# An encoder layer on one core: the attention's output product as seven block products in place of eight, with the sums in DRAM replanned

## The chip, the cores and the metric

The kernel runs on one core of one Trainium2 chip. The metric is device time in microseconds (us), the median of several runs of the same program. The program's text runs once and is scheduled ahead of time into one instruction stream per engine: PE (matmuls), DVE and ACT (elementwise work), POOL and SP (here mostly issuing transfers). Streams run in order and wait for each other by semaphores.

## The reference

A bidirectional encoder layer on 512 tokens of width 1024, all in float32: a state-space branch and a gated branch are merged, then comes cross-attention to 256 memory tokens, then a SwiGLU feed-forward part (FFN) of width 2816 and a last norm. What the change touches is the end of the attention:

```python
def memory_cross_attention(hn, memn, w_q, w_k, w_v, w_o):
    q = (hn @ w_q).reshape(bsz, seq, XATTN_HEADS, XATTN_HEAD_DIM)      # 4 heads of 256
    ...
    p = jax.nn.softmax(s, axis=-1)
    o = jnp.einsum('bhlm,bmhd->blhd', p, v).reshape(bsz, seq, D_MODEL)
    return o @ w_o                                                     # w_xo, 1024 x 1024

h = h + memory_cross_attention(rms_norm(h, xattn_norm_g[i]), memn, w_q[i], w_k[i], w_v[i], w_xo[i])
h = h + swiglu(rms_norm(h, ffn_norm_g[i]), w_gate[i], w_up[i], w_down[i])
```

## The kernel before

**Products.** PE multiplies a reduced float32 type. Every operand is therefore split into a high part (a cast, on ACT) and a low part (the rest, by a subtraction on DVE); `split` does both, at lines 85 and 86. `mm3` (line 358) then issues three matmuls: high by high, high by low, low by high. Weights are split on the chip as they come: a load of 512 KB by SP into `wraw` (three buffers), then `whi` on ACT and `wlo` on DVE (three buffers each).

**The plan.** All weight pieces stand in one list, `plan`, in the order of their use. `next_w` hands out the next piece, starts the load of the piece three places ahead (`LOADS`) and splits up to two places ahead (`SPLITS`). Program order comes from this; a scheduler then orders each engine's stream by its own estimate of when things are ready.

**Strassen's products before the change.** `w_proj_b`, `w_q`, most of `w_gate` and `w_up` (in units of 512 columns) and `w_down` are already computed as block products of seven for eight: tokens, rows and columns of the weight are halved, seven products of sums of blocks are formed instead of eight of blocks, and their results are added up. Four of the seven need a sum of weight blocks. For `w_proj_b`, `w_q` and `w_down` these sums (`bsum`, `qsum`, `dsum`) are made in DRAM, long before they are used: `plan_sums` hangs each job on two places of the plan, at the first a copy of one block by SP (line 274), some places later a second transfer, issued by POOL, that adds the other block onto it (line 275). The numbers in `plan_sums([...])` are these places and distances.

**`w_xo` before.** It is an ordinary product. `values` makes one head's attention output (two tiles `po`) and splits it into `ot_hi` and `ot_lo`. `tokm(w_xo, 0, ...)` computes the first 512 columns for all four token tiles, with the values of heads 1 to 3 hooked in between its weights. The loops over `t0` behind it compute the other 512 columns, two token tiles at a time. `add_evac` adds each result onto `h`, sums its squares on ACT, and for the second half starts the FFN's norm of that token tile (`feat_norm`, `norm_feat`): two scalings `xs` (line 512), transposes on PE (`ptr`, line 520), and the split into `fn`.

**The FFN's start** takes tokens 0 and 1 first (`gate_part(0, T0)`, a unit's first product, `gate_part(1, T0)`, a unit's second), then tokens 2 and 3. T0 and T1 are the halves of the tokens, K0 and K1 those of the rows.

Of the kernel before, what the change touches and what calls it, by code (L numbers as in the profile page):

```python
# [9 lines left out]
F32 = mybir.dt.float32  # L10
# [42 lines left out]
def hybrid_layer_kernel(  # L53
# [173 lines left out]

    def plan_units(units, down):
# [28 lines left out]
    def plan_sums(places):  # L257
# [1141 lines left out]
    def values(hd, p_hi, p_lo):  # L1399
        for dt_ in range(2):  # L1400
# [4 lines left out]
            split(ot_hi[:, 2 * hd + dt_, :], ot_lo[:, 2 * hd + dt_, :], ps)  # L1405
# [49 lines left out]
    ot_lo = slot("E", (P, KD, T), F32R, "ot_lo")  # L1455
    values(0, *pts.pop(0))
    probs2 = scores(2)
    probs3 = scores(3)
    turn(1, probs1)

    def second():
        values(1, *pts.pop(1))
        turn(2, probs2)
        turn(3, probs3)

    def last_two():
        for i in (2, 3):
            values(i, *pts.pop(i))

    g_f = gain(ffn_norm_g[0], "g_f")  # L1470
    ot = (ot_hi, ot_lo)
    fn_hi, fn_lo = token_slot("fn", AWAY)
    fn = (fn_hi, fn_lo)

    tokm(w_xo, 0, ot, KD, add_evac(0, 1, None), hooks={1: second, 2: last_two})
# [6 lines left out]
    full = fp.tile([P, KD, T], F32, tag="full", name="full", bufs=1)  # L1482


    fin = add_evac(1, 1, feat_norm(g_f, fn_hi, fn_lo, full))
    held = []
    for t0 in (0, 2):
        ps = {t: bank(f"pt{t - t0}") for t in (t0, t0 + 1)}
        for wi in range(2):
            if t0 == 0:  # L1490
                held.append((wi,) + next_w(w_xo, 2 * wi, 2, 512, 512))
            for t in ps:
                tok_block(ps[t], t, held[wi:wi + 1], ot, 2, slice(0, 512), wi == 0, False)
            tick(2.7)
        if t0 == 0:
            held += [(wi,) + next_w(w_xo, 2 * wi, 2, 512, 512) for wi in (2, 3)]
        for t in ps:
            tok_block(ps[t], t, held[2:4], ot, 2, slice(0, 512), False, True)
            fin(t, ps[t])
            tick(2.7)  # L1500
# [308 lines left out]
```

## Time and profile before

| | |
|---|---|
| median of 3 runs | 892.44 us (892.33 to 893.95) |
| the profiled execution | 893.12 us, of which its span is 891.3 us |
| PE, busy share of the span | 99% |
| DVE, ACT, POOL | 72%, 55%, 12% |
| granted TensorE clock, mean | 0.997 |
| DMA | 165.36 MB, 186 GB/s on average |

A row of the chain of waits has start, length and what the chain was in. A row of the timeline has engine, line, operation, output and inputs, shape and count, and in brackets the idle time ahead of it with what ended it. A group row ends in busy us, mean ns of one, and idle time ahead of the group with what ended it. PEld is the loading of a matmul's stationary side, beside PE.

### The profile page before, as it was taken

How to read it: one execution, taken by the hardware profiler on the slowest of the kernel's cores; microseconds unless marked ns; L12 is line 12 of the kernel's file. 1: busy time of each engine (PE TensorE's matmuls, PEld its weight loads, DVE VectorE, ACT ScalarE, POOL GpSimd, SP SyncE). 2: the span in 40 equal slices, each digit the busy share in tenths (PEclk: the TensorE clock that was granted, in tenths of full speed). 3: DMA queues.
4: the chain of work that ended last, by engine and by line, in shares of the span. 5: the costliest groups of instructions: out<-in, count | busy, mean ns of one | idle time of the engine just before them, and what ended most of it. 6: DMA issues, size and time to landing. Idle time of an engine off the chain costs nothing.

```text
span 891.3 us, 14796 instructions
## 1 busy us (share of the span) xinstructions
PE 881.1 (99%) x5744; PEld 788.0 (88%) x5744; DVE 642.5 (72%) x1048; ACT 487.4 (55%) x714; POOL 106.9 (12%) x165
## 2 busy tenths in 40 slices
PE   9999999999999999999999999999999999999996
PEld 6788888888889998889899978999999999988875
DVE  5697653889847368658856836676878777899875
ACT  5743994244396254347656534645555455655664
POOL 1005301111032111001001001101121111000010
PEclk9999999999999999999999999999999999999998
DMA  8667456978533789834579747627899999356672
GB/s 255 196 189 182 114 155 177 189 191 190 159 87 84 212 285 268 288 117 140 168 221 256 194 103 197 166 81 181 213 237 233 216 225 249 95 167 207 204 230 102
DMA packets 118408, 165.36 MB, mean 186 GB/s; under 512 B 11825, under 2 KB 84161, under 8 KB 118210
## 3 DMA queue, kind: packets, MB, share of 16 engines
q1 hardware_dynamic: 97474, 135.74, 47.9%
q0 software_dynamic: 20576, 28.15, 19.9%
q8 instruction: 45, 0.74, 0.3%
q10 hardware_dynamic: 288, 0.52, 0.2%
q14 instruction: 25, 0.20, 0.1%
HBM read 157.61 MB, written 46.63 MB: 229 GB/s over the span
## 4 chain that ended last, share of the span: by engine, by line
PE 97%; DMA 1%; SPq 1%; ACT 0%; DVE 0%; issue 0%; POOLq 0%; ACTq 0%
PE pf L358 26%; PE pt L358 17%; PE px L1110 12%; PE dx L358 6%; PE pq L1110 6%; PE dq L358 3%; PE pv L1110 3%; PE bx L1110 3%; PE qx L1110 2%; PE dv L358 2%; PE pz L871 2%; PE pk L814 2%; PE bq L1110 1%; PE qv L1110 1%; PE psc L358 1%; PE qq L1110 1%
## 5 line engine op out<-in xcount | busy, mean ns | idle before, releaser
L86 DVE TENSOR_TENSOR wlo<-wraw,whi 128x1024 fp32r<-128x1024 f32 (+1 forms) x145 | 172.2, 1189 | 101.2 <-ACT whi L85 101.0
L85 ACT CAST whi<-wraw 128x1024 fp32r<-128x1024 f32 (+1 forms) x145 | 148.6, 1026 | 152.2 <-PE pf L358 44.0
L358 PE MATMUL pf<-xn,whi 128*128 128x512 f32 x448 | 139.6, 391 | 0.0
L358 PEld LDWEIGHTS pf<-xn,whi 128*128 128x128 f32 x448 | 83.7, 188 | 17.0
L358 PE MATMUL pf<-xn,wlo 128*128 128x512 f32 x224 | 87.3, 390 | 0.0
L1110 PE MATMUL px<-fn,whi 128*128 128x256 f32 x480 | 83.4, 277 | 0.0
L1110 PEld LDWEIGHTS px<-fn,whi 128*128 128x128 f32 x480 | 72.7, 188 | 0.2
L85 ACT CAST whi<-b 128x1024 fp32r<-128x1024 f32 x40 | 42.2, 1055 | 50.4 <-PE px L1110 27.4
L86 DVE TENSOR_TENSOR wlo<-b,whi 128x1024 fp32r<-128x1024 f32 x40 | 48.9, 1223 | 27.0 <-ACT whi L85 27.0
L1110 PE MATMUL px<-fn,wlo 128*128 128x256 f32 x240 | 66.4, 277 | 0.0
L1110 PE MATMUL pq<-s,whi 128*128 128x256 f32 x320 | 55.0, 276 | 0.0
L358 PE MATMUL dx<-whi,s 128*128 128x512 f32 x170 | 53.4, 390 | 0.4 <-DVE h L1734 0.4
L85 ACT CAST whi<-t 128x1024 fp32r<-128x1024 f32 x30 | 31.6, 1054 | 35.6 <-PE pv L1110 12.4
L86 DVE TENSOR_TENSOR wlo<-t,whi 128x1024 fp32r<-128x1024 f32 x30 | 36.7, 1225 | 19.7 <-ACT whi L85 19.7
L358 PEld LDWEIGHTS pf<-xn,wlo 128*128 128x128 f32 x224 | 42.1, 188 | 8.7
L1110 PEld LDWEIGHTS pq<-s,whi 128*128 128x128 f32 x320 | 48.3, 188 | 0.0
L1110 PEld LDWEIGHTS px<-fn,wlo 128*128 128x128 f32 x240 | 45.1, 188 | 0.0
L358 PE MATMUL pt<-whi,xn 128*128 128x512 f32 x128 | 43.7, 412 | 0.7 <-ACT xn L85 0.7
L1110 PE MATMUL pq<-s,wlo 128*128 128x256 f32 x160 | 44.2, 276 | 0.0
L358 PEld LDWEIGHTS dx<-whi,s 128*128 128x128 f32 x170 | 31.8, 188 | 7.5 <-issue 0.8
L358 PE MATMUL dx<-wlo,s 128*128 128x512 f32 x85 | 33.0, 390 | 0.0
L275 POOL DMA_DIRECT2D dsum<-in_w_down_dram x12 | 13.3, 1105 | 162.4 <-DMA dsum<-in_w_down_dram 162.4
(453 smaller groups left out, 2296.8 us busy)
## 6 DMA issues: line engine op xcount, KB each, us to landing
wraw<-in_w_in_dram SPq DMA_DIRECT2D x36, 512.0 KB, 4.7
dsum<-in_w_down_dram SPq DMA_DIRECT2D x20, 512.0 KB, 5.4
wraw<-dsum SPq DMA_DIRECT2D x20, 512.0 KB, 4.1
b<-in_w_gate_dram SPq DMA_DIRECT2D x15, 512.0 KB, 5.4
b<-in_w_up_dram SPq DMA_DIRECT2D x15, 512.0 KB, 5.3
wraw<-in_w_down_dram SPq DMA_DIRECT2D x15, 512.0 KB, 4.4
dsum<-in_w_down_dram POOLq DMA_DIRECT2D x10, 512.0 KB, 8.1
dsum<-dsum POOLq DMA_DIRECT2D x10, 512.0 KB, 8.5
```

Of the source, the lines that this page charges most:

```text
L85: hi = nc.scalar.copy(dst_hi, src)
L86: lo = nc.vector.tensor_tensor(dst_lo, src, dst_hi.bitcast(F32), ALU.subtract)
L275: plan[j + step][1].append((0, lambda d=dst, x=more: nc.gpsimd.dma_start(d, x, accum_op=ALU.add)))
L358: m = nc.tensor.matmul(ps, a[x], b[y], start=start and i == 0, stop=stop and i == 2, skip_group_check=free)
L814: nc.tensor.matmul(ps[32 * j:32 * j + 32, q, :], bd[i][:, g].rearrange("p d c -> p (d c)"), lc(es[i], g), start=(i == 0), stop=False, tile ...
L871: nc.tensor.matmul(ps[:, g, :], wt[:, g, :], u[:, o * GO + g, :], start=True, stop=True)
L1110: nc.tensor.matmul(ps[:, j, :], a[x], b[y], start=start and j == k == i == 0, stop=k == 3 and i == 2, skip_group_check=True)
```

## The change

`w_xo` becomes a block product of seven for eight over all 1024 columns. `plan_xo` puts 14 pieces of 512 KB into the plan in place of 8: for each of the products 1 to 7 two pieces (`c` = 0, 1) of 256 rows by 512 columns. Products 1, 2 and 3 read blocks of `w_xo`; 4 to 7 read sums `xsum`, made in DRAM by eight new jobs of `plan_sums`. The places of all sums are written anew: the last two of `w_q`'s come earlier, `w_xo`'s take the places that held `w_q`'s last and `w_down`'s first, three of `w_down`'s are beside `w_xo`, 15 in the FFN's units and six (those of product 4) at the places of `w_down` itself. The order of `w_down`'s sums of products 6 and 7 is exchanged.

On the side of the tokens, `values` now copies `po` to a float32 tile `of` on ACT, and `attention_part` makes the operands of the products from it: after heads 0 and 1 those of products 1 and 7, after heads 2 and 3 those of 6, 5, 4, 2 and, later, 3, with four sums or differences per pair of heads on DVE. `xo_product` multiplies one piece with two token tiles; products 1 and 7 stand between the heads' values. `onto` adds a finished product onto two token tiles of one half of `h`. The FFN's norm of tokens 0 and 1 is started after product 4, that of tokens 2 and 3 after product 3, the last. The memory of the keys (`kt_hi`, `kt_lo`) takes the operands of products 5 and 6.

```diff
+    XSRC = {1: (0, 0), 2: (1, 0), 3: (1, 1)}
+    xsum = {q: dp.tile([P, KD // 2, 512], F32, name=f"xsum{q}") for q in (4, 5, 6, 7)}
+    XO = ((1, 0), (7, 0), (1, 1), (7, 1), (6, 0), (5, 0), (6, 1), (5, 1), (4, 0), (4, 1), (2, 0), (2, 1), (3, 0), (3, 1))
+    def xo_block(i, j, c):
+        return block(w_xo, 4 * i + 2 * c, 2, 512 * j, 512)
+    def plan_xo():
+        for q, c in XO:
+            ...
+                got["raw"] = wp.tile([P, 2, 512], F32, tag="raw", name="wraw", bufs=3)
+                nc.sync.dma_start(got["raw"], xo_block(*XSRC[q], c) if q in XSRC else xo_sum(q, c))
...
-        for q, i, jc, more in ((5, 0, 0, lambda c: down_block(0, 1, c)), (7, 0, 1, lambda c: down_block(1, 1, c)),
-                               (6, 1, 1, lambda c: down_sum(5, c)), (4, 1, 0, lambda c: down_sum(6, c))):
+        for q, first, more in ((5, (0, 0), lambda c: xo_block(0, 1, c)), (7, (0, 1), lambda c: xo_block(1, 1, c)),
+                               (6, (1, 1), lambda c: xo_sum(5, c)), (4, (1, 0), lambda c: xo_sum(6, c))):
+            for c in range(2):
+                jobs.append((xo_sum(q, c), xo_block(*first, c), more(c)))
+        for q, i, jc, more in ((5, 0, 0, lambda c: down_block(0, 1, c)), (6, 1, 1, lambda c: down_sum(5, c)),
+                               (7, 0, 1, lambda c: down_block(1, 1, c)), (4, 1, 0, lambda c: down_sum(6, c))):
...
-    plan_tok(w_xo, 0, KD)
-    for i in range(4):
-        plan_block(w_xo, 2 * i, 2, 512, 512, place=(None, None, 2, 4)[i])
+    plan_xo()
...
-    plan_sums([(5, 3), (7, 3), (9, 2), (13, 5), (14, 5), (16, 4)] + [(18 + 2 * i, 3) for i in range(8)] +
-              [(51 + 2 * i, 2) for i in range(4)] + [(85 + 3 * i, 3) for i in range(3)] +
-              [(95 + 2 * i, 2) for i in range(3)] + [(122 + 4 * i, 4) for i in range(16)])
+    plan_sums([(5, 3), (7, 3), (9, 2), (13, 5), (14, 5), (16, 4)] + [(18 + 2 * i, 3) for i in range(5)] +
+              [(i, 3) for i in (28, 29, 31, 32, 34)] + [(51 + 2 * i, 2) for i in range(4)] +
+              [(i, 3) for i in (67, 74, 82, 87, 91, 95, 99)] + [(124 + 4 * i, 4) for i in range(15)] +
+              [(184 + 5 * i, 4) for i in range(6)])
...
-            split(ot_hi[:, 2 * hd + dt_, :], ot_lo[:, 2 * hd + dt_, :], ps)
+            nc.scalar.copy(of[:, 2 * hd + dt_, :], ps)
+        attention_part(hd)
...
+    xops = {1: ot_q(K0, T1), 2: ot_q(K1, T1), 4: ot_q(K1, T0), 7: ot_q(K0, T0), 3: ot_q(K0, T1)}
+    def attention_part(hd):
+        ...
+        if hd < 2:
+            operand(1, a11)
+            s3_ = np_.tile([P, 2, 256], F32, tag="ev", name="s3", bufs=2)
+            nc.vector.tensor_tensor(s3_, a11, a21, ALU.subtract)
+            operand(7, s3_)
+            return
+        nc.vector.tensor_tensor(a21, a21, a22, ALU.subtract)
+        nc.vector.tensor_tensor(a11, a21, a11, ALU.subtract)
+        operand(6, a11)
+        operand(5, a21)
+        operand(4, a22)
+        operand(2, a12)
+        nc.vector.tensor_tensor(a12, a12, a11, ALU.add)
+        later(2, lambda: operand(3, a12))
...
-    tokm(w_xo, 0, ot, KD, add_evac(0, 1, None), hooks={1: second, 2: last_two})
+    ox = [bank("ox0"), bank("ox1")]
+    xo_product(ox, 1, 0, True, False)
+    values(1, *pts.pop(1))
+    turn(2, probs2)
+    oy = [bank("oy0"), aux("oy1")]
+    xo_product(oy, 7, 0, True, False)
+    values(2, *pts.pop(2))
+    turn(3, probs3)
+    xo_product(ox, 1, 1, False, True)
+    onto(ox, 2, 0, ALU.add)
+    values(3, *pts.pop(3))
+    xo_product(oy, 7, 1, False, True)
+    onto(oy, 0, 1, ALU.subtract)
+    oq = [bank("oq0"), bank("oq1")]
+    xo_product(ox, 6, 0, False, False)
+    xo_product(oq, 5, 0, True, False)
+    xo_product(ox, 6, 1, False, True)
+    onto(ox, 0, 1, ALU.subtract)
+    xo_product(oq, 5, 1, False, True)
...
+    onto(oq, 0, 1, ALU.add)
+    onto(ox, 0, 0, ALU.add)
+    ...
+    onto(ox, 2, 1, ALU.subtract)
+    xo_product(oy, 4, 0, False, False)
+    xo_product(oy, 4, 1, False, True)
+    ...
+    for t in range(2):
+        hs = h[:, t, HALF[0]]
+        nc.vector.tensor_tensor(hs, hs, oy[t], ALU.add)
+        half_done(t, 0)
+        to_fn(t, hss[:, 1, t, :])
+    ov = [bank("ov0"), bank("ov1")]
+    xo_product(ov, 2, 0, True, False)
+    xo_product(ov, 2, 1, False, True)
+    onto(ov, 2, 0, ALU.add)
+    ...
+    for t in range(2):
+        for c in range(2):
+            xo_product(oq, 3, c, False, c == 1, ws[c], (t,))
+        hs = h[:, 2 + t, HALF[1]]
+        nc.vector.tensor_tensor(hs, hs, oq[t], ALU.add)
+        half_done(2 + t, 1)
+        to_fn(2 + t, hss[:, 1, 2 + t, :])
```

More of the change, by code (lines that the diff above doesn't have):

```diff
@@ L1455, in hybrid_layer_kernel, with operand, xo_product, onto @@
     ot_lo = slot("E", (P, KD, T), F32R, "ot_lo")
+    of = slot("B", (P, KD, T), F32, "of")
+    ot_q = lambda ks, ts: (ot_hi[:, ks, ts], ot_lo[:, ks, ts])
+    xops = {1: ot_q(K0, T1), 2: ot_q(K1, T1), 4: ot_q(K1, T0), 7: ot_q(K0, T0), 3: ot_q(K0, T1)}
+    def attention_part(hd):
+        u = slice(2 * (hd % 2), 2 * (hd % 2) + 2)
+        lw = slice(u.start + 4, u.stop + 4)
+        a11, a12, a21, a22 = (of[:, k, t] for t in (T1, T0) for k in (u, lw))
+        def operand(q, src):
+            split(xops[q][0][:, u], xops[q][1][:, u], src)
+        if hd < 2:
[12 more added lines that the diff above has]
+        later(2, lambda: operand(3, a12))
+    g_f = gain(ffn_norm_g[0], "g_f")
+    def xo_product(ps, q, c, start, stop, w=None, ts=(0, 1)):
+        hi, lo = w or next_w(w_xo, q, c)
+        a = xops[q]
+        for t in ts:
+            tsl = slice(t * P, (t + 1) * P)
+            for k in range(2):
+                mm3(ps[t], (a[0][:, 2 * c + k, tsl], a[1][:, 2 * c + k, tsl]), (hi[:, k, :], lo[:, k, :]),
+                    start and k == 0, stop and k == 1, True)
+        tick(1.35 * len(ts))
+    def onto(ps, t0, half, op):
+        for t in range(2):
+            hs = h[:, t0 + t, HALF[half]]
+            nc.vector.tensor_tensor(hs, hs, ps[t], op)
+    def half_done(t, half):
+        sum_sq(hss[:, 1, t, half:half + 1], h[:, t, HALF[half]])
     values(0, *pts.pop(0))
@@ L1458, in hybrid_layer_kernel @@
     probs3 = scores(3)
+    for q, nm in ((5, "kt_hi"), (6, "kt_lo")):
+        s_ = ap_.tile([P, KD, M], F32R, name=nm).rearrange("p (i k) t -> p i k t", i=2)
+        xops[q] = s_[:, 0], s_[:, 1]
     turn(1, probs1)
[L1461 to L1473, printed above, removed]
-    tokm(w_xo, 0, ot, KD, add_evac(0, 1, None), hooks={1: second, 2: last_two})
+    ox = [bank("ox0"), bank("ox1")]
[17 more added lines that the diff above has]
+    xo_product(oq, 5, 1, False, True)
     at.close()
@@ L1482, in hybrid_layer_kernel @@
     full = fp.tile([P, KD, T], F32, tag="full", name="full", bufs=1)
[L1485 to L1500, printed above, removed]
+    onto(oq, 0, 1, ALU.add)
+    onto(ox, 0, 0, ALU.add)
+    for t in range(2):
+        half_done(t, 1)
+    onto(ox, 2, 1, ALU.subtract)
+    xo_product(oy, 4, 0, False, False)
+    xo_product(oy, 4, 1, False, True)
+    fn_hi, fn_lo = token_slot("fn", AWAY)
+    fn = (fn_hi, fn_lo)
+    to_fn = feat_norm(g_f, fn_hi, fn_lo, full)
+    for t in range(2):
+        hs = h[:, t, HALF[0]]
[6 more added lines that the diff above has]
+    onto(ov, 2, 0, ALU.add)
+    for t in (2, 3):
+        half_done(t, 0)
+    ws = [next_w(w_xo, 3, c) for c in range(2)]
+    for t in range(2):
+        for c in range(2):
[4 more added lines that the diff above has]
+        to_fn(2 + t, hss[:, 1, 2 + t, :])
     s3 = np_.tile([P, 4, 256], F32, tag="gain", name="s3", bufs=2)
```

5 lines of the change are left out of this document (added).

## The prediction

> **What bounds the kernel now.** I read the page first, then the chain of waits in order of time, then busy times by stretch, then single rows of the engines beside the change.
>
> ```profile
> span 891.3 us, 14796 instructions
> ...
> PE 881.1 (99%) x5744; PEld 788.0 (88%) x5744; DVE 642.5 (72%) x1048; ACT 487.4 (55%) x714; POOL 106.9 (12%) x165
> ...
> q1 hardware_dynamic: 97474, 135.74, 47.9%
> q0 software_dynamic: 20576, 28.15, 19.9%
> ...
> PE 97%; DMA 1%; SPq 1%; ACT 0%; DVE 0%; issue 0%; POOLq 0%; ACTq 0%
> ```
>
> PE is busy in 99% of the span and is 97% of the chain that ends last. Taking matmuls away therefore takes time away, as long as PE is fed. Over the whole span DVE has 28% to spare, but that is a mean over stages. The question is what it has to spare where `w_xo` stands:
>
> ```profile
> 497.00:505.70 8.70, 8.70 (x67) 8.15 (x66) 8.44 (x21) 5.70 (x16) 0.86 (x1) 1.00 0.78 221
> 505.70:564.00 58.30, 57.36 (x270) 46.38 (x269) 32.67 (x57) 27.73 (x54) 5.31 (x6) 1.00 0.52 136
> 564.00:577.00 13.00, 13.00 (x112) 12.95 (x112) 9.10 (x13) 6.99 (x13) 1.87 (x2) 1.00 0.72 212
> ...
> 784.00:820.00 36.00, 36.00 (x162) 29.84 (x161) 34.36 (x41) 21.08 (x27) 0.81 (x1) 1.00 0.66 193
> 784.00:884.00 100.00, 99.58 (x448) 82.33 (x447) 83.67 (x104) 59.73 (x82) 5.09 (x7) 1.00 0.63 190
> ```
>
> Each row is a stretch, its length, then busy us of PE, PEld, DVE, ACT and POOL, granted clock, DMA share and GB/s. `w_xo` runs from 505.7 to 564; the 8.7 us before it are the last softmax work, the 13 us behind it the start of the FFN. In these 80.0 us DVE is busy for 8.44 + 32.67 + 9.10 = 50.2 us and ACT for 40.4. The last two rows are the `w_down` stage: DVE there reaches 34.36 of 36 us (95%) without PE waiting.
>
> **Part 1: the product.** Now `w_xo` is 4 token tiles by 8 row tiles by 2 column halves by 3 = 192 matmuls of 128x512. Seven block products of 2 token tiles by 4 row tiles by 3 are 168. So 24 go. Their spacing and the stalls beside them:
>
> ```profile
> 513.72 0.59 ACT p_hi L85
> 514.30 0.50 ACT ot_hi L85
> ...
> 523.89 0.59 ACT ot_hi L85
> ...
> 536.38 17.32 PE pt L358 x76
> 553.70 0.87 PE ptr L520 x8
> ...
> 808.74 14.96 PE dv L358 x66
> ```
>
> The row of 76 matmuls gives 17.32 / 76 = 0.228 us for one, so 24 x 0.228 = **5.47 us less on PE**. The three ACT rows are the only places of this stretch where the chain leaves PE: 0.59 + 0.50 + 0.59 = **1.68 us** in which PE waits for the attention output to be split straight before it is used. In the changed order another block product stands between a head's values and their first use, so I take these as gone, too. The floor of the stretch is thus 80.0 - 5.47 - 1.68 = 72.9 us.
>
> **Part 2: what DVE and ACT get for it.** The changed program's order has, on DVE, 6 more weight splits of 128x1024 (14 instead of 8), 6 more operand splits, 8 sums of attention outputs and 10 more additions onto `h` (18 instead of 8), these 24 all of 128x512. ACT gets 6 casts of 128x1024 and 14 copies or casts of 128x512.
>
> ```profile
> 537.99 2.36 DVE L86 TENSOR_TENSOR s<-wraw,s 128x1024 fp32r<-128x1024 f32 x2 [0.26 <-ACT s L85]
> 540.27 1.88 DVE L1294 TENSOR_TENSOR h<-h,pt 128x512 f32<-128x512 f32 x3
> ...
> 553.99 1.42 DVE L512 SCALAR_TENSOR_TENSOR xs<-h,r,g_f 128x512 f32<-128x512 f32 x2 [1.02 <-POOL r L497]
> ...
> L86 DVE TENSOR_TENSOR wlo<-wraw,whi 128x1024 fp32r<-128x1024 f32 (+1 forms) x145 | 172.2, 1189 | 101.2 <-ACT whi L85 101.0
> L85 ACT CAST whi<-wraw 128x1024 fp32r<-128x1024 f32 (+1 forms) x145 | 148.6, 1026 | 152.2 <-PE pf L358 44.0
> ```
>
> The two of 128x1024 begin at 537.99 and the next operation at 540.27, so back to back they start 1.14 apart; their row is 2.36 long, so each one's end is reported 0.08 past its successor's start (1.22 for one). The three of 128x512 then start (1.88 - 0.08) / 3 = 0.60 apart and last 0.68. DVE therefore gains 6 x 1.14 + 24 x 0.60 = **21.2 us**: 50.2 + 21.2 = 71.4 us of DVE work in a stretch whose floor is 72.9 us, a share of 98%. ACT gains at most 6 x 1.03 + 14 x 0.59 (the `p_hi` row above) = 14.4 us, 54.8 in all, and is not the limit. So the saved PE time is only to be had as far as DVE can be packed.
>
> The Trainium skill (VectorE: DVE Perf Modes, "The DRAIN you can't avoid") says that the next DVE operation doesn't start until the pipe of the one before is empty. By whole durations the addition would be 6 x 1.22 + 24 x 0.68 = 23.6 us. The trace has it otherwise where nothing is waited for (0.60 apart, not 0.68), and I use 21.2.
>
> Where the packing fails first follows from the order. When block product 4 ends, PE has products 2 and 3 left as cover: 48 matmuls x 0.228 = 10.9 us, and 16 transposes at 0.87 / 8 = 0.109, 1.7 us: 12.7 us. On DVE stand, between that end and the split of the second token tile that the FFN's first matmuls read: five of 128x1024 (5.7), eight of 128x512 (4.8), two pairs `xs` (2 x 1.35), one wait for `r` of 1.0, together 14.2 us, and one weight split that it is behind by (1.1). 15.3 - 12.7 = **2.6 us of stall at the start of the FFN**. Ahead of it I count 0.4 us where head 1's second `p_lo` comes later (three operand operations in place of two), and 0.6 us where the weight of product 5's second half waits for a buffer that the order frees late, because PE puts off half of product 6. New stalls: **3.6 us**, bounded by 0 (perfect packing) and by what the stretch would be at the 84% that DVE has over the whole `w_down` stage: 71.4 / 0.84 = 85.0 us, 12.1 over the floor. I stay near the lower end, since 95% is held for 36 us above and my sum comes to 71.4 / 76.5 = 93%.
>
> **Part 3: the sums in DRAM.** Eight jobs for `w_xo` come in, each a copy by SP and an accumulating transfer by POOL; `w_down`'s move back.
>
> ```profile
> wraw<-qsum SPq DMA_DIRECT2D x6, 512.0 KB, 5.4
> wraw<-in_w_xo_dram SPq DMA_DIRECT2D x6, 512.0 KB, 6.4
> ...
> wraw<-dsum SPq DMA_DIRECT2D x15, 512.0 KB, 4.1
> wraw<-in_w_down_dram SPq DMA_DIRECT2D x10, 512.0 KB, 4.4
> ```
>
> These are transfers with their us to landing: the first two between 452 and 500, beside `w_down`'s sums, the last two between 800 and 884, with no sum beside them. From the two queue rows, 512 KB cost 0.479 x 891.3 x 0.524 / 135.74 = 1.65 us of all engines on q1 and 0.199 x 891.3 x 0.524 / 28.15 = 3.3 us on q0: a job costs 4.95 us. One job of `w_down`'s every 5 loads (13 us) adds 0.37 to the `w_down` stage's DMA share of 0.63: 1.0. A raw buffer there serves every third load; one round is landing + cast 1.03 + split 1.19 + about 0.4 of issue and handing over, and a product of 66 matmuls (14.96 us) needs two full rounds of a buffer: it binds from a landing of 14.96 / 2 - 2.6 = 4.9 us. At 4.1 to 4.4 it doesn't; beside a job it is 5.4 to 6.4. Landings will be mixed, so I take **0.6 us**, bounds 0 and 2 x (6.4 - 4.9) x 5 products = 15.
>
> Earlier, two of `w_q`'s sums move ahead, beside `w_in`'s last columns, where each load feeds 24 matmuls (5.5 us) and a landing of 6.4 us stays under the three loads that are kept ahead: nothing, bounds -0.5 and 0.5. SP gets `w_proj_a`'s first load ahead of the four `ygt` loads:
>
> ```profile
> 318.44 1.77 SPq L1222 DMA_DIRECT2D ygt<-yd  x4
> 320.25 0.43 SPq L1245 DMA_DIRECT2D gat<-gad  x1
> 320.73 0.47 SPq L137 DMA_DIRECT2D wraw<-in_w_proj_a_dram  x1
> ```
>
> If that load waits for its buffer until about 320.3, `ygt` and all behind it in the queue shift by 2.3 us. The `w_glu` products that read it take one tile per 12 matmuls (2.7 us) in the new order and hide most of that: **0.4 us**, bounds 0 and 2.3. In the units DMA jobs stand as close as before: nothing, bounds -0.5 and 0.5. The loads of `w_xo`, 14 instead of 8, run at a DMA share that was 0.52: covered, and if the cover were gone a late load would cost up to its landing beyond 4.9, 1.5 us.
>
> **The sum** is made against the profiled execution, 893.12 us (span and 1.8 around it): 893.12 - 5.47 - 1.68 + 3.6 + 0.6 + 0.4 = 890.6. That execution stands 0.7 above the median of 892.44, so **889.9** against the median.
>
> **The rivals.** 0.2% is 1.8 us here, about what a measurement of this kernel can tell from no change: faster ends at 890.7, slower begins at 894.2.
> 1. *DVE packs to 97%*, as in the 8.44 of 8.70 us above: the stretch is 73.6 us, 3 us less than forecast, about 887; without the other stalls 886. For it: its work is known long ahead; against: the norm's short chain over ACT, DVE and POOL (the 1.02 us of `r`).
> 2. *DVE's operations cost more than I charge*, their whole durations (73.8 us of work) at the same 93%: 79.1 us, 2.6 more than forecast, 892.5: no change. The 1.88 us for three speak against it. The Trainium skill's rule quoted above (VectorE: DVE Perf Modes, "The DRAIN you can't avoid") would give this.
> 3. *DVE ends the stretch, and loosely*: below 88% the stretch takes over 81 us, and the kernel is slower. The place is from head 2's values to the FFN's first matmuls, where softmax, operand sums, `h` and weights wait for each other in one queue. At 86%: 71.4 / 0.86 = 83.0, 6.5 more than forecast: 896.4.
> 4. *`w_down` becomes bound by its loads*: at a landing of 6.0 us, 2 x 1.1 x 5 products less 2.7 us that two ready weights give = 8.3: 897.6. It decides against the change from about 5.5 us. Against it: between 452 and 500 PE lost nothing at such landings (but it had scores to fill in).
> 5. *It doesn't do what it says*: the 24 matmuls are gone by the program's order, so only a sum that comes late and stalls all the products could undo it: 892.
>
> **How the numbers follow.** Forecast with DVE between 92.5 and 96%: 0.42, of it all under 890.7. Rival 1: 0.13. Together faster 0.55. Rival 2 0.16 and rival 5 0.03: same 0.19. Rival 3 0.16 and rival 4 0.10: slower 0.26. The forecast's own range is 887.8 to 890.7. The range for 8 in 10 takes in rival 1 down to 886.5, rival 2, and rival 3 down to a share of 86% or most of rival 4: 896.5.
>
> **What would show it.** Right: 168 instead of 192 matmuls of this product; DVE near 71 us in the stretch from the last scores to the FFN's second token half, at over 90%; the chain leaving PE at the FFN's start for DVE; `w_down`'s products still 14.96 us each. Wrong: PE waits for `wlo` or for the sums throughout the seven products; `w_down` products longer than 15 us with loads ending the wait; or a stretch below 74 us.

## The result, and the profile after

The change makes the kernel slower: 904.27 us median (902.26 to 908.10, 4 runs) against 893.15 (892.33 to 893.95, 4 runs), a ratio of 1.0132 (95% interval 1.0102 to 1.0161). The forecast was 889.9, with a range up to 896.5. Repeated later, it gave 904.93 (1.0116; 1.0083 to 1.0148). The profiled execution took 902.26 us.

From the page of the kernel after, the span, the busy times and the chain that ended last by engine:

```profile
span 900.5 us, 14859 instructions
PE 880.5 (98%) x5720; PEld 782.8 (87%) x5720; DVE 662.8 (74%) x1078; ACT 499.0 (55%) x734; POOL 114.8 (13%) x173
PE 79%; DMA 8%; DVE 6%; ACT 3%; issue 2%; SPq 1%; POOL 0%; POOLq 0%; ACTq 0%; DVEq 0%
```

The 24 matmuls are gone (5744 to 5720), yet PE is as "busy" as before (881.1): a matmul behind a short wait is drawn longer, so that this share hides stalls (the matmul `idle` in the experiments is drawn with 396 to 398 ns, and with 499 behind a wait). The chain shows them: PE fell from 97% to 79%, DMA and DVE took 14% together.

Where the time went is read best from the start of a stage's first matmul in PE's order of time. The six stretches are: to the first matmul of `w_proj_b` (`bx`), from there to `w_q` (`qx`), from there to the last score (`psc`), from there to the first unit (`pq`: attention outputs, `w_xo`, start of the FFN), the units, and `w_down` to the end. Where no sum was moved, traces agree within 0.1 us in the units, 0.4 up to `w_q` and 1.1 in `w_q`. The first stretch scatters by 4 us, all of it in about the first 30 us, in which PE waits for the first loads. The two traces of the changed kernel differ by 1.0 us up to `w_q`, 1.2 in `w_q` and 2.0 in the stretch of `w_xo`, and `w_q` differs by 2.2 between experiments 15 and 16 below, with its sums at the same places; a difference of that size in one trace is no finding.

| us | to w_proj_b | to w_q | w_q | w_xo, FFN start | units | w_down |
|---|---|---|---|---|---|---|
| before | 261.7 | 190.7 | 53.2 | 87.6 | 190.7 | 107.4 |
| after | 261.2 | 194.3 | 54.6 | 85.4 | 190.8 | 114.1 |
| after, second trace | 262.7 | 193.3 | 53.4 | 87.4 | 190.8 | 114.0 |

The product gained 2.2 us in the first trace and 0.2 in the second. Most of this difference is the clock: in the second trace the granted clock was 0.59 from 566 to 569 us and 0.94 from 569 to 577, which by (1 - clock) times length is up to 1.7 us; in the first it stayed at 1.00. `w_down` lost 6.7, the stretch up to `w_q` 3.6, `w_q` 1.4. The chain of the kernel after, in order of time (start, us, what), cut to its pieces on engines other than PE at these places:

```profile
290.38 1.19 POOL qsum L301
291.70 1.32 POOL kd L861 x3
293.21 8.30 DMA kd<-ks
...
306.99 1.51 DMA yd<-y
...
336.42 1.05 ACT whi L85
337.53 1.22 DVE wlo L86
338.76 1.07 DVE glu L1256
...
463.74 8.06 DMA wraw<-qsum
...
544.65 1.22 DVE wlo L86
545.89 6.39 DMA wraw<-in_w_xo_dram
552.38 1.06 ACT whi L85
553.46 1.23 DVE wlo L86
557.71 1.33 DVE xs L537 x2
560.08 1.23 DVE s L86
561.33 5.01 DMA wraw<-in_w_up_dram
...
803.24 5.77 DMA wraw<-in_w_down_dram
...
829.73 8.74 DMA wraw<-dsum
...
857.07 5.41 DMA wraw<-dsum
...
870.43 6.80 DMA wraw<-dsum
```

Read from the top: one of `w_q`'s sums that were moved ahead is accumulated at 290.4, and the small transfer of `kd` beside it needs 8.30 us (the transfers of `kd` at this place took 5.1 to 5.5 us in the kernel before); what waits for it in SP's queue (`yd`) is late. At 336 a weight of `w_proj_a` is cast behind `w_glu`'s first result: the moved queue entries made the order on PE bring all four `w_glu` tiles together (first result 8.9 us after the start of `w_glu`, where it was 6.7). At 463 a load of `w_q` takes 8 us beside a sum of `w_xo`. Around 550 weights and the norm stand in one line of waits. In `w_down` the long pieces are loads that land late.

The stretch of `w_xo` in the same columns as before (stretch, length, PE, PEld, DVE, ACT, POOL, clock, DMA share, GB/s):

```profile
501.50:510.14 8.64, 8.64 (x65) 8.09 (x63) 8.45 (x18) 6.23 (x16) 1.14 (x1) 1.00 0.79 203
510.14:562.80 52.66, 51.14 (x239) 41.36 (x238) 47.31 (x79) 35.11 (x65) 3.56 (x4) 1.00 0.61 172
562.80:579.00 16.20, 13.85 (x117) 13.43 (x117) 12.92 (x22) 11.11 (x20) 1.99 (x3) 1.00 0.72 233
```

That is 77.5 us in place of 80.0 (forecast 76.5), with 68.7 us of DVE (forecast 71.4), a share of 89%.

### The profile page after: what moved, and what is told of

The parts are those of the page before. It is cut to its first block, busy times and chain, and to the rows that moved or that the text cites. A ratio compares the mean times of both kernels' runs of the same rounds, so it can differ in the third digit from the quotient of the medians.

```text
span 900.5 us, 14859 instructions
## 1 busy us (share of the span) xinstructions
PE 880.5 (98%) x5720; PEld 782.8 (87%) x5720; DVE 662.8 (74%) x1078; ACT 499.0 (55%) x734; POOL 114.8 (13%) x173
## 4 chain that ended last, share of the span: by engine, by line
PE 79%; DMA 8%; DVE 6%; ACT 3%; issue 2%; SPq 1%; POOL 0%; POOLq 0%; ACTq 0%; DVEq 0%
PE pf L383 25%; PE pt L383 12%; PE px L1135 12%; PE pq L1135 6%; PE dx L383 3%; PE pv L1135 3%; DMA wraw<-dsum 3%; DVE wlo L86 2%; PE pz L896 2%; PE qx L1135 2%; ACT whi L85 1%; PE po L383 1%; PE qq L1135 1%; PE bq L1135 1%; PE pk L839 1%
## 5 line engine op out<-in xcount | busy, mean ns | idle before, releaser
L86 DVE TENSOR_TENSOR wlo<-wraw,whi 128x1024 fp32r<-128x1024 f32 (+1 forms) x153 | 181.9, 1190 | 97.7 <-ACT whi L85 96.2
L85 ACT CAST whi<-wraw 128x1024 fp32r<-128x1024 f32 (+1 forms) x153 | 156.5, 1026 | 165.6 <-PE pf L383 44.5
L1135 PEld LDWEIGHTS pq<-s,wlo 128*128 128x128 f32 x160 | 30.1, 188 | 0.0
```

The source lines that it names most:

```text
L85: hi = nc.scalar.copy(dst_hi, src)
L86: lo = nc.vector.tensor_tensor(dst_lo, src, dst_hi.bitcast(F32), ALU.subtract)
L1135: nc.tensor.matmul(ps[:, j, :], a[x], b[y], start=start and j == k == i == 0, stop=k == 3 and i == 2, skip_group_check=True)
```

## The experiments

In all tables below the columns are those of the first one, each row from one trace. Times are medians in us; in brackets stands the median of the kernel before, run beside it. A filler is a matmul whose result nobody uses.

**1. The replan alone.** The kernel before with the other sums at the changed places (its `w_down` sums also in the changed order):

```diff
-[(18 + 2*i, 3) for i in range(8)] + [(51 + 2*i, 2) for i in range(4)] + ... + [(122 + 4*i, 4) for i in range(16)]
+[(18 + 2*i, 3) for i in range(5)] + [(i, 3) for i in (28, 29, 31, 32, 34)] + [(i, 3) for i in (91, 95, 99)]
+ + [(118 + 4*i, 4) for i in range(15)] + [(178 + 5*i, 4) for i in range(6)]
```

> The kernel before, its w_xo product untouched, with the changed kernel's places for the other sums (two of w_q's ahead, six of w_down's beside w_down) and no w_xo sums. Theory T (the loss is the replan: 3.4 us up to w_k, 6.8 in w_down): 893.2 + 10.2 = about 903. Rival (the loss is the seven products and the DVE work that they bring): 894 or less.

902.68 (before 893.45), ratio 1.0106 (1.0081 to 1.0131). Without one block product of `w_xo` the replan costs most of what the change costs: 1.06% of 1.32%.

**2. `w_down`'s sums out of `w_down`:** `[(124 + 4*i, 4) ...15] + [(184 + 5*i, 4) ...6]` becomes `[(122 + 3*i, 4) for i in range(21)]`.

> The changed kernel with w_down's last 21 sums all beside the gate and up units (one per three weights in place of one per four), none beside w_down. Theory T (the sums beside w_down starve its loads: its stage took 113.9 us instead of 107.0): the w_down stage is back at 107 us and the kernel at about 897.4, 6.8 below the changed one. Rival (a sum costs what it costs wherever it stands): the units grow by what w_down loses, total about 904.

899.11 (893.45), ratio 1.0059 (1.0041 to 1.0078).

**3. `w_q`'s sums back:** the first 16 places as before, `w_xo`'s at 55, 57, 60, 63, 67, 74, 82, 87.

> The changed kernel with the sums of w_q where they were before (two of them again beside w_glu), w_xo's last ones of the early group beside w_out. Theory T (the two sums moved ahead delay kd and yd on POOL and SP, and w_glu's tiles come in another order: 1.3 + 2.15 us): w_glu to w_k is as before and the kernel at about 900.9. Rival (the early loss is the bytes of the eight new sums, which are all still there): 904.

909.69 (893.45), ratio 1.0169 (1.0133 to 1.0204): far off, though the stage in question is mended.

**4. The product alone:**

```diff
-nc.sync.dma_start(got["raw"], xo_block(*XSRC[q], c) if q in XSRC else xo_sum(q, c))
+nc.sync.dma_start(got["raw"], xo_block(*XSRC.get(q, (0, 1)), c))      # and no job of w_xo's
```

> The seven products with every other sum at its place of before, and no sums for w_xo: products 4 to 7 read plain blocks of w_xo instead, so this part of the output is another product of the same size and cost. It shows what the product alone is worth. Theory T (the stretch from w_xo to the FFN gains 2.4 us): 890.7. By the prediction's own sum (-5.5 - 1.7 + 3.6): 889.6. Rival (the product itself costs, on DVE): 893.2 or more.

900.21 (893.45), ratio 1.0071 (1.0055 to 1.0088).

| us | to w_proj_b | to w_q | w_q | w_xo, FFN start | units | w_down |
|---|---|---|---|---|---|---|
| 1 replan alone | 261.5 | 195.5 | 53.2 | 87.6 | 190.7 | 115.6 |
| 2 sums in units | 262.4 | 194.3 | 53.6 | 86.9 | 190.8 | 108.3 |
| 3 w_q's sums back | 265.0 | 190.5 | 54.9 | 86.7 | 197.6 | 113.3 |
| 4 product alone | 261.5 | 190.5 | 53.2 | 87.1 | 197.6 | 108.2 |

Two losses are settled by rows that go with one edit each. `w_down` takes 113.3 to 115.6 us where sums stand beside it and 107.4 to 108.3 where at most the last, half-size one does, and the units don't grow by the six sums that they take over (190.8). The exchanged order of products 6 and 7 is no part of it: experiment 2 has it still. From `w_proj_b` to `w_q` it is 193.3 to 195.5 us with `w_q`'s sums ahead and 190.5 with them back; in experiment 3 the transfers of `kd` take 3.9 to 4.3 us again, and `w_glu`'s first result comes as early as before. For `w_down`, the DMA issues of the kernel after (name, queue, count, KB, median us to landing) and its waits (engine, line, for what: us in all, times, longest), then the same wait in experiment 2:

```profile
wraw<-dsum SPq DMA_DIRECT2D x20, 512.0 KB, 4.7
dsum<-in_w_down_dram SPq DMA_DIRECT2D x4, 512.0 KB, 6.0
dsum<-dsum POOLq DMA_DIRECT2D x4, 512.0 KB, 7.5
...
ACT whi L85 <- DMA wraw<-dsum: 19.1, 12, 5.1
ACT whi L85 <- DMA wraw<-in_w_down_dram: 14.5, 8, 4.1
```

```profile
ACT whi L85 <- DMA wraw<-dsum: 6.1, 4, 2.7
```

The median landing rose from 4.1 to 4.7 only, still under the 4.9 at which the prediction saw the ring bind; but single loads beside a sum take 5.4 to 8.7 us, and the longest wait for one is 5.1 us in place of 2.7. Four full-size sums more than before fall into this stage: 1.7 us each.

But in 3 and 4 something new appears: 6.9 us lost in the units, to which no edit was made. Their chain shows it, first the product alone, then (from experiment 7 below, the same kernel with one filler moved) the usual rhythm:

```profile
592.45 2.83 PE pq L1126 x24
595.27 8.48 PE px L1126 x72
```

```profile
592.74 2.72 PE pq L1126 x24
595.46 8.16 PE px L1126 x72
```

72 matmuls of 128x256 take 8.48 us (117.8 ns apart) in place of 8.16 (113.3), all through the units, by the same instructions. What differs is how this stream begins. The kernel has one filler matmul `idle` of 128x512 ahead of the gate's second token half. In the product alone PE stood still right before it (`fn` was late) and it is drawn longer; the query by tile gives duration as min/median/max and the waits:

```profile
L1132 PE MATMUL idle<-fn x1: 499/499/499, 577.8 to 577.8; 128*128 128x512 f32 x1
...
  ACT fn L85: 1.9, 2
```

In the kernels before and after it took 396 to 398 ns and PE waited for nothing.

**5. The filler left out of the kernel before** (`idle_product(ops[1][0], fn_hi)` deleted):

> The kernel before without its one filler matmul ahead of the gate's second token half. Theory P (the filler sets the rhythm of the 128x256 matmuls behind it): 117.8 ns in the units, about 7 us longer, 900. Rival (in the kernel before PE doesn't wait there, so the rhythm holds without it): 893.2.

902.54 (893.42), ratio 1.0088 (1.0065 to 1.0111); the units take 197.6 us.

**6. Three fillers in the product alone:**

> As the product alone (products 4 to 7 of w_xo read plain blocks, so that part of the output is another product of the same cost), but with three filler matmuls of 128x512 in place of one ahead of the gate's second token half. In the product alone PE waited for fn straight before the one filler, and from there to the end of the units its 128x256 matmuls started 117.8 ns apart in place of 113.6. Theory P (a wait of PE right at the start of the stream leaves it in the slower rhythm, and some matmuls behind the wait bring it back): 113.6 ns, units 6.9 us shorter, total about 893.4. Rival (the rhythm comes from something else, such as the place of the code): 117.8 ns still, about 900.7.

894.31 (893.42), but in two heaps: six of ten runs at 892.65 to 894.35, four at 900.16 to 903.47; in the profiled one the units took 190.8.

**7. The filler moved** behind the two `gate_part(i, T1)`, where PE waits for nothing:

> The product alone (products 4 to 7 of w_xo read plain blocks, so that part of the output is another product of the same cost), with its one filler matmul moved behind the gate's second token half, where PE waits for nothing. Theory P2 (one filler that runs without a wait before it turns the rhythm of what follows): 113.6 ns in w_up and all units in every run, 893 to 894.5, where the filler behind the wait gave 117.8 ns and 900.2. Rival (any filler behind a wait of the same stage leaves it to chance): some runs at 900.

893.65 (894.03), ratio 1.0001 (0.9987 to 1.0015), all ten runs between 892.43 and 896.87. So there are two lasting rhythms of this stream, and how PE comes to the filler decides between them: without a filler it is the slower one (5), with one behind a wait the slower one or either (4, 6), with one behind matmuls that don't wait the faster one (7). The traces show the filler at work. In the kernel before, 24 matmuls ahead of it take 2.83 us (118 ns apart) and 144 behind it 16.34 (113.5). In the product alone those ahead of the wait are 113.3 ns apart and those behind the filler 117.8: a filler behind a wait can also turn the faster rhythm into the slower. In experiment 7 the matmuls ahead of the moved filler are already 113.3 apart, so its trace alone can't tell the new place of the filler from its absence behind the wait. That of experiment 14 below, with the filler at the same new place, can: 48 matmuls ahead of it are 118 ns apart and 96 behind it 113.3.

```profile
577.80 5.66 PE pf L374 x48
583.46 0.23 PE idle L1132
583.69 10.88 PE pf L374 x96
```

Why PE has two rhythms was not found, and the product alone without any filler was not tried. And the product alone, with its sums for nothing and the rhythm right, gains nothing.

**8. Mended places** (experiments 2 and 3 joined, `w_xo`'s last sums beside `w_v`, three fillers) and **9. the eight sums of attention outputs on POOL** (`nc.vector` to `nc.gpsimd`) in it:

> The seven products with sums placed so that none of the found losses should occur: w_q's sums as before, w_xo's beside w_glu, w_out, w_k and w_v alone, w_down's last 21 beside the units, three fillers ahead of the gate's second half. Theory T (the product gains 1.2 to 2.4 us and all the rest was the places): 891 to 892.3. Rival (the eight sums of w_xo cost 1 to 3 us wherever they stand, as their 24.6 us of DMA engines would suggest): 894 or more.

> As the mended places, and the eight sums of attention outputs done by POOL (13% busy) in place of DVE. Theory D (DVE's queue is what makes PE wait from w_xo to the FFN, 4.6 us in the changed kernel): 4.8 us of DVE work less in that stretch, its stalls fall by about 2 us, total 2 us below the mended places. Rival L (the ring of three raw buffers and the landing of the loads set it): the same as the mended places within 0.5. Rival S (POOL takes longer for a sum, and the operands of products 4 to 6 wait for it): slower.

901.97 and 902.58 (893.42), ratios 1.0090 (1.0061 to 1.0119) and 1.0095 (1.0066 to 1.0124), scattered over 8 us, so the rhythm was again left to chance. The stages of the two traces:

| us | to w_proj_b | to w_q | w_q | w_xo, FFN start | units | w_down |
|---|---|---|---|---|---|---|
| 8 mended places | 261.3 | 192.1 | 56.6 | 88.0 | 190.8 | 107.4 |
| 9 sums on POOL | 261.9 | 191.5 | 55.3 | 87.1 | 197.6 | 107.4 |

`w_xo`'s sums close together beside `w_v` cost 1 to 1.6 us there, and `w_q` loses 2 to 3.4. With POOL, the waits at the FFN's start fell from 2.9 us in one piece to 0.7, but product 6 waited up to 2 us for its operands, since POOL takes 1.3 to 2.1 us for a sum of 0.6 on DVE. It neither proves nor disproves that DVE is the limit.

**10. The changed kernel again:**

> The changed kernel once more, for the spread of its times and a second trace. Theory T (losses from the places of the sums: about 3 us up to w_k, 1.4 in w_q, 6.8 in w_down, and 2.2 gained in between): the same stages again within 1.5 us, total 902 to 906; runs above 906 would be those in which the units have the 117.8 ns rhythm. Rival (the stages of the first trace were chance): other stages lose.

904.93 (894.03), ratio 1.0116 (1.0083 to 1.0148). Up to `w_q` and in `w_down` the same losses; both traces have the 113.3 ns rhythm, so it is no part of the loss in them. Whether the runs above 906 have the other one is open.

**11. Four sums on POOL**, those that are not needed soon, on experiment 7:

> As the filler moved (the product alone, plain blocks in products 4 to 7), and four of the eight sums of attention outputs on POOL: those that nothing waits for soon (heads 0 and 1 for product 7, the operand of product 3). Theory D (DVE's queue makes PE wait from w_xo to the FFN): 2.4 us of DVE work less, the stretch from the last scores to the units shrinks by 1 to 2.4 us, total 1 to 2 below the filler moved. Rival A (ACT's order at the FFN's start sets the wait: the Silu table load ahead of the split of fn): no change in the stretch.

896.62 (894.03), ratio 1.0033 (1.0018 to 1.0047), 3 us slower than 7; the stretch is 91.0 us. POOL worked on one sum for 4.49 us beside a busy DVE. ACT's cast of product 3's operand waited 4.0 us for it, and the weight of product 4, which was needed sooner, stood behind that cast in ACT's queue. From the timeline of POOL:

```profile
532.64 4.49 POOL L1500 TENSOR_TENSOR of<-of 128x512 f32<-128x512 f32 x1 [6.05 <-DVE of L1495]
```

**12 to 14. What takes the product's gain?** On experiment 7 one suspect each was taken away: the three sums of `w_down`'s beside `w_xo`; the eight sums of attention outputs; two of the 14 weights.

> As the filler moved (the product alone, plain blocks in products 4 to 7), and the three sums of w_down's that stand beside w_xo moved into the units. In the filler moved, DMA was at a share of 1.05 and more from 540 to 558 us, a load of w_gate took 13.0 us to land, and PE lost 3.7 + 1.7 us there. Theory L (what PE waits for at the end of w_xo is DMA: w_xo's loads, the first unit's, and the sum): the share falls, that load lands in 8 us or less, the stretch is 1.5 to 3 us shorter, total 891 to 892.2. Rival D (DVE's queue issues the load late and sets the end): within 0.5 of the filler moved, 893.7.

> As the filler moved (the product alone, plain blocks in products 4 to 7), with the eight sums of attention outputs left out: the operands are split from plain blocks, so the output of this part is another product of the same cost, with 4.8 us less on DVE. Theory D (DVE's queue is the limit from the last scores to the FFN): the stretch is 2 to 4.8 us shorter, total 889 to 892. Rival L (DMA is the limit at the end of w_xo): at most 1 us, 892.7 to 893.7.

> As the filler moved (the product alone, plain blocks in products 4 to 7), and product 3 reads the two weights of product 2, so two of w_xo's 14 loads, casts and splits at its end are left out; PE's matmuls are the same. Theory W (at the end of w_xo each weight feeds only 12 matmuls, 2.7 us, and three raw buffers with a landing of 5 to 8 us and 2.3 us of cast and split cannot keep up, so weights are what PE waits for): product 3's waits (0.9 to 2.0 us each) go and the first weights of the FFN come earlier; the stretch is 2.5 to 4 us shorter, total 890 to 891.2. Rival N (the norm's chain from h over ACT, DVE and POOL to the transposes sets the end): product 3's waits go, the FFN's start waits as long as they were, total within 1 us of 893.65.

893.90 (894.06), 892.73 (894.06) and 895.42 (893.71); ratios 0.9997 (0.9979 to 1.0015), 0.9988 (0.9969 to 1.0007), 1.0018 (1.0004 to 1.0031). No gain that was expected came. In the last one product 3 did not wait at all, and PE waited 4.2 us in one piece at the FFN's start instead; the granted clock behind that wait was 0.53 (562.0 to 565.6), and the matmuls there start 1.2 us late in all for it. The stretch remains what it was, 87.1 to 88.1 us. The chain of experiment 7, then that of the two weights less, shows the same piece:

```profile
544.24 12.99 DMA wraw<-in_w_gate_dram
```

```profile
545.49 12.41 DMA wraw<-in_w_gate_dram
```

**15. The whole change mended** (`w_q`'s sums as before, `w_xo`'s thinly from 55 to 87, `w_down`'s one at 91 and 23 in the units, filler moved), and **16. the same with the first unit's loads later** (`(7, 5, 5)` to `(5, 4, 3)` weights ahead):

> The whole change with what the runs taught: w_q's sums as before, w_xo's eight thinly from w_glu to w_q, w_down's not beside w_xo and not beside w_down but 23 of 24 in the units, the filler behind the gate's second token half. By the parts: product alone with this filler 893.7, minus what the sums beside w_xo cost there (0 to 2), plus 0.3 to 1.7 that loads lose beside w_xo's sums in w_q: 892 to 895.4, against 893.2 to 894 before. Rival (the units, at one sum per 2.9 weights, become bound by loads): 897 or more.

> The mended version (places and filler), with three loads and the accumulation of the first unit asked for two weights later, so that they do not run beside w_xo's last loads (DMA share 1.0 and more there). Theory W: w_xo's last weights and w_gate's first land sooner, the stretch is 1 to 2 us shorter, total 893.3 to 894.3 where the mended version took 895.3. Rival (the end of w_xo is not bound by DMA, as the sum taken away there showed): 895.3.

895.27 (894.06), ratio 1.0010 (0.9992 to 1.0029), and 894.99 (893.71), ratio 1.0017 (1.0004 to 1.0030). All of the 11 us but about one are mended, none of the two is faster than the kernel before.

**17 and 18. Loads eased together, then the sums left out too:**

```diff
 # 17: on experiment 7
-XO = (..., (4, 0), (4, 1), (2, 0), (2, 1), (3, 0), (3, 1))
+XO = (..., (4, 0), (4, 1), (2, 0), (2, 1))                  # product 3 uses product 2's weights
 # no sum of w_down's beside w_xo; the first unit's loads (5, 4, 3) weights ahead
 # 18: also
-s3_ = ...; nc.vector.tensor_tensor(s3_, a11, a21, ALU.subtract); operand(7, s3_)
+operand(7, a21)                                            # and so for the other six
```

> As the filler moved (the product alone, plain blocks in products 4 to 7), with all that eases the loads at the end of w_xo together: product 3 reads product 2's two weights (two loads less), no sum of w_down's beside w_xo, and three loads and the accumulation of the first unit asked for two weights later. In the runs before, a load of w_gate took 12.4 to 13.0 us to land and PE's wait only moved from product 3 to the FFN's start. Theory L (landings at this joint set the end of the stretch): that load lands in 6 us or less, the stretch from the last scores to the units is 3 to 5 us shorter, total 889 to 891. Rival N (the chain of h, norm and splits on DVE and ACT sets it): the stretch within 1 us of 87.6, total 893 to 895.

> As the loads eased, and the eight sums of attention outputs left out as well (4.8 us less on DVE; operands split from plain blocks, another product of the same cost). Theory J (two limits of near the same length stand at this joint, DVE's queue and the landings, so that easing one uncovers the other): here the forecast gain of the product appears, the stretch is 3.5 us or more shorter than 87.6, total 888.5 to 890.5. Rival N (the norm's chain alone): within 1.5 us of the loads eased.

893.76 (893.35), ratio 0.9996 (0.9979 to 1.0013), and **888.48** (893.35), ratio **0.9936** (0.9912 to 0.9960).

| us | to w_proj_b | to w_q | w_q | w_xo, FFN start | units | w_down |
|---|---|---|---|---|---|---|
| 7 filler moved | 261.3 | 190.5 | 53.2 | 87.6 | 190.7 | 107.9 |
| 12 no sum beside | 262.2 | 190.3 | 53.6 | 87.6 | 190.8 | 107.4 |
| 13 no operand sums | 261.1 | 190.5 | 53.2 | 87.1 | 190.7 | 107.9 |
| 14 two weights less | 261.8 | 190.5 | 53.9 | 88.1 | 190.7 | 107.6 |
| 15 whole, mended | 262.4 | 190.5 | 56.1 | 88.3 | 190.8 | 107.4 |
| 16 first unit later | 261.2 | 190.5 | 53.9 | 88.7 | 190.8 | 107.4 |
| 17 loads eased | 261.1 | 190.6 | 54.3 | 87.7 | 190.8 | 107.5 |
| 18 and sums out | 263.0 | 190.5 | 53.7 | 80.6 | 190.7 | 107.5 |

Easing DVE alone (13) gives 0.5 us, easing the loads alone (17) nothing, both together (18) 7.0. But 17 also lost clock: over its whole stretch the granted clock is 0.96, in 7, 13 and 18 it is 1.00. Behind a wait of 3.6 us at 556 its matmuls run at about half the clock until 567, and start 2.3 us late in all for it. Without that, easing the loads would have shown some 2 us (an estimate: 87.6 - (87.7 - 2.3)). The stretches by tens of us, of 7, 17 and 18 in this order (same columns as above):

```profile
520.00:535.00 15.00, 15.00 (x67) 12.18 (x66) 14.95 (x22) 9.86 (x15) 1.17 (x1) 1.00 0.55 145
535.00:545.00 10.00, 10.00 (x46) 8.24 (x45) 10.00 (x15) 4.61 (x8) 1.14 (x1) 1.00 0.86 295
545.00:555.00 10.00, 7.12 (x35) 5.15 (x34) 7.17 (x14) 5.46 (x12) 2.46 (x3) 1.00 1.12 276
```

```profile
520.00:535.00 15.00, 15.00 (x67) 12.13 (x66) 14.80 (x22) 10.81 (x17) 0.00 (x0) 1.00 0.26 89
555.00:565.00 10.00, 5.48 (x30) 4.69 (x29) 9.96 (x17) 7.43 (x17) 1.07 (x2) 0.76 0.20 61
```

```profile
520.00:535.00 15.00, 15.00 (x67) 12.31 (x66) 12.01 (x16) 9.28 (x16) 0.00 (x0) 1.00 0.31 104
545.00:555.00 10.00, 10.00 (x52) 8.46 (x51) 8.88 (x16) 5.49 (x9) 2.48 (x3) 1.00 1.11 298
555.00:565.00 10.00, 9.90 (x74) 9.17 (x73) 9.05 (x17) 8.49 (x18) 1.10 (x2) 1.00 0.48 146
```

In 7 DVE is full from 520 to 545 (14.95 of 15, 10.00 of 10) while DMA's share is 0.55 up to 535: the three raw buffers are given back by DVE's splits, so a full DVE holds the loads back. When it catches up, `w_xo`'s last loads, `w_gate`'s first and the first unit's stand in DMA together (share 1.12), one takes 13 us, and DVE in turn is idle for 28% of 545 to 555. I read the stall as two queues that hold each other up in turn; this reading is argued from the rows, and no run separates a held load from a slow one. In 17 the loads come in time and DVE (9.96 of 10) is late with `h`, norm and splits at 555; the clock of 0.76 in that row fell behind this wait. In 18 DVE has slack from 520 on, and PE is fed throughout. That both limits bind within the same few us is shown by 13, 17 and 18: easing either alone leaves 4.8 us or more of the seven, even with 17's clock put right. How the seven divide between them, and the clock that falls behind a wait, was not settled.

## Why the prediction was wrong, step by step

In spans the forecast was 888.8 (891.35 less 2.55); the trace shows 900.5, 11.7 more. By the stages: `w_down` 6.2, the two stretches up to `w_q` 2.75 together, `w_q` 1.4, the product 1.4.

- *Part 1, the floor (-5.47 and -1.68):* right, as a floor. With both limits eased the stretch is 7.0 us shorter than before, where 7.15 was worked out.
- *Part 2, new stalls of 3.6 us:* mis-sized, and in part not for the reason given. Against their usual spacing, PE's matmuls start 2.5 us late in this stretch before and 5.6 after (7.8 in the second trace, 1.6 of it at the lower clock; 7.5 in the product alone); the forecast amounts to 2.5 - 1.7 + 3.6 = 4.4. That the stretch came out within 1 us of the forecast in the first trace (77.5 against 76.5) is partly luck: DVE had 2.7 us less to do than was worked out, and the second trace is 2.0 us longer. The place at the FFN's start was right, product 5's weight was not: it is product 3's weights. DVE's spacing was right too: the six additions onto `h` from 541.07 on take 3.66 us, (3.66 - 0.08) / 6 = 0.60 each, though they read PSUM, so rival 2 (whole durations, the rule quoted from the Trainium skill) falls. That section of the Trainium skill adds that a next operation which is not held starts earlier, and the 0.60 agrees with that. What the step missed is that it took DVE's share as the only limit and "the loads of `w_xo`, 14 instead of 8" as covered because DMA's share was 0.52. DVE frees the buffers that loads wait for. In the kernel after it was busy for 24.37 of the 25 us from 520 to 545, with DMA at 0.55 and 0.54; in the next 10 us DMA's share was 1.04.

```profile
541.07 3.66 DVE L1527 TENSOR_TENSOR h<-h,ox 128x512 f32<-128x512 f32 x6
```

- *Part 3, `w_down`'s sums (+0.6, bounds 0 and 15):* the step that failed most. It measured 6.7. Rival 4 was this mechanism at 8.3 us, with a chance of 0.10, set aside because the landings would be "mixed" and PE had lost nothing at 5.4 to 6.4 us beside `w_q`. But a ring of three (the raw buffers, used in turn) doesn't work by the median: four loads of 5.4 to 8.7 us in the chain were enough (in the second trace five of 5.6 to 6.7). The note in brackets, that PE had scores to fill in there, may well be why nothing was lost there (not tested), and should have counted against the comparison.
- *Part 3, `w_q`'s two sums moved ahead (nothing, bounds -0.5 and 0.5):* false; 2.6 to 4.8 us over four traces. It was priced by the loads of weights alone. Beside them run the small transfers of `kd` and `yd`, which PE's recurrence waits for, and the order on PE changed for `w_glu`. The price of `ygt` (+0.4, bounds 0 and 2.3) lies in the same stretch and can't be told apart.
- *`w_q` (not priced):* 1.4, 0.2 and 0.4 us in the three traces with these places (the third is experiment 2); 0.7 to 3.4 with `w_xo`'s sums at others, 0 to 1.0 without any. The loads there were judged by the landing before (5.4), with `w_down`'s sums beside them; what makes a sum of `w_xo`'s in their place dearer was not tried.
- *The units (0):* right at 190.8, in both traces. The rhythm that cost other variants 6.9 us was not foreseen; in these two traces PE comes to the filler without a wait, and as nobody had looked at that, it is luck.
- *Rivals:* 1 and 5 did not happen. 3 (below 88%, over 81 us) did not either: 89% and 77.5 us in the first trace. The sign was lost by rival 4 and by an edit that had no rival at all.

## What to carry to other kernels

Price a moved transfer by everything that lands beside it, small dependent ones first, and by the worst landing that a short ring of buffers meets, not by the median; the sums that were to fill idle DMA beside `w_down` cost three times what the product gained in the same trace (6.7 against 2.2 us). When an engine that frees load buffers goes from half busy (12.3 of 25 us before) to nearly 100%, look for loads that bunch up behind it even if DMA's mean share is low; here easing one of the two showed little until both were eased. Read the granted clock of a stage before comparing two traces of it: one wait can cost more at the lower clock behind it. After any edit compare the spacing of an untouched stream of matmuls: a stage that is a few per cent slower with the same instructions may have been thrown into another rhythm by a wait ahead of it.

## What the runs showed of the hardware

- **Two rhythms of one matmul stream.** Pairs of weight load and 128x256 matmul run 113.3 or 117.8 ns apart for 190 us on end, at a granted clock of 1.00 in both. One 128x512 filler decided it: by the times of the runs, the longer spacing came in four of four runs of the kernel before without the filler; with it behind a wait in four of four (one filler) or four of ten (three); with it behind matmuls that don't wait in none of ten.
- **The clock can fall after short waits.** In the product alone three matmuls started 0.98, 0.47 and 2.01 us behind the ones before them, all within 5.2 us, and the next matmuls of 128x512 started 0.43 us apart in place of 0.227 (the two windows are the last wait and what follows):

```profile
551.70:553.70 2.00, 0.33 (x3) 0.09 (x1) 2.00 (x4) 1.42 (x2) 0.00 (x0) 1.00 1.16 240
553.70:558.00 4.30, 4.24 (x12) 3.35 (x13) 3.10 (x6) 3.06 (x8) 0.00 (x0) 0.60 1.08 276
```

The granted clock of 0.60 makes the three waits cost another 1.6 us (eight matmuls by 0.20). The Trainium skill (TensorE: Matmul & The Clock Gate, Part 1) has the clock halved after one idle window of about 3.4 us. The wait of 3.6 us in experiment 17 agrees with that; in the product alone no single wait was that long. Nor do waits of this size decide alone: in the kernel after, waits of 1.38 and 2.42 us, 4 us apart, left the clock at 1.00; in its second trace waits of 1.41 and 2.41 us at the same places brought it down (the first row from the first trace, the second from the second):

```profile
566.00:572.00 6.00, 5.85 (x51) 5.63 (x49) 4.78 (x10) 4.40 (x10) 1.06 (x2) 1.00 0.44 133
566.00:569.00 3.00, 3.00 (x17) 3.00 (x18) 3.00 (x5) 3.00 (x7) 0.00 (x0) 0.59 0.13 27
```

The Trainium skill also says there that this window runs freely, so that where a wait falls in it would matter. The two traces agree with that, but shorter waits ahead of these two differ between them as well, and no run here separates the two.
- **POOL beside a busy DVE** took 1.3 to 4.5 us for a 128x512 sum, where DVE starts one every 0.60 us. The Trainium skill (GPSIMD Engine Reference, 1. Specifications) has POOL's SBUF interfaces shared with VectorE and contended by its instructions with two SBUF inputs; the splits around the row of 4.49 us are such, which agrees, and no run here separates it.
